# Opening of a hybrid layer: from a normed and transposed x to a transposed x whose norm factor comes later

## The chip, the cores and the metric

The kernel runs on one core of one Trainium2 chip. The metric is device time in microseconds. The kernel before takes 2043.03 us, the median of three runs (2042.36 to 2048.4).

## The reference

For x of 512 tokens by 2048 channels the layer is, with every matrix in float32:

```python
h = rmsnorm(x, norm_w)                      # x * rsqrt(mean(x*x) + eps) * norm_w, per token
z, xbc, dt_f, dt_b, q_a, kv_a, z_attn, g_ssm, g_attn = split(h @ w_in)
xbc = silu(dwconv(xbc, conv_w, conv_b))     # a centred convolution over four tokens
y = ssd_scan(...) both directions + d_skip * xs
y = group_rmsnorm(y * silu(z))
o = attention(q_a, kv_a) * silu(z_attn)
merged = sigmoid(g_ssm) * (y @ w_proj_ssm) + sigmoid(g_attn) * (o @ w_proj_attn)
out = rmsnorm(x + merged @ w_out, final_norm_w)
```

Since the norm's factor is one number per token, h @ w_in is that factor times (x * norm_w) @ w_in. The convolution mixes tokens, so there the factor must be in before it.

## The kernel before, in words

Each float32 operand is split into a high part (a cast to the matmul's format) and a low part (what the cast left over). A product is three matmuls: high by high, high by low, low by high. A matmul has a 128 x 128 stationary side and 512 columns. A weight chunk is 128 x 1024 numbers, 512 KB. SyncE's queue (SP) loads it, ScalarE (ACT) casts it to `wh`, VectorE (DVE) makes `wl`, and TensorE (PE) uses it for 24 matmuls in a plain gemm and 12 in a gate product. `wraw`, `wh` and `wl` have three buffers each.

TensorE's instructions run in the order in which the program is written. The other engines' order, and that of the DMA issues on their queues, is made by a scheduler from priorities: a gate weight's load stands up to 160 steps ahead, its split 60.

The program's stages are these.

1. Opening (L195 to L235). x is loaded in eight pieces, token by token (L208); ScalarE squares and sums each (L210); the factor is made for each group of 128 tokens (L185 to L191); x is scaled (L218, L220); 64 transposes turn it channel by channel (L225). From the turned tiles come `h_h` (L229) and `h_l` (L230), the high and low part of h with norm_w in.
2. Seven gemms on h by plain chunks (L168 to L170): `dtp`, then six for the first group of xbc. Between them `h_sums` (L723 to L743) rebuilds quarters of h from both parts and makes S1, S2, S3 and S4, the sums that the gates need, in two halves (`q`). `dt_make` (L279 to L303) makes the time steps out of `dtp`.
3. Three gates (`wz`, `wgs`, `wga`), each in two column pairs by a Strassen-Winograd scheme of seven half-size products in the order P1, P5, P6, P2, P3, P7, P4 (lines L576 to L578). A product takes four chunks and 48 matmuls. P1's chunks X are loaded by SP; when P1 has split one, POOL adds a second block of weights onto it by an accumulating DMA (L503), which makes T1, P5's operand. Y is another block; X plus Y (L670) is P6's operand, and X plus a further block (L674) is that of P4, called T4. S3 is loaded back from memory behind P5 (L445), and x21 at the end of the last pair.
4. The state scan with the other plain gemms beside it, then attention.
5. Three projections, `wps`, `wpa` and `wo`, by the same scheme; the operands S1 to S4 and x11 to x22 of the next one are loaded and split during the last products of the one before.

Row names: `xt` is x by tokens, `P` a product's bank, `wl` a low part of a weight, `T_wps` a stored sum of weights, `o_S` a stored operand of the next projection.

## Time and profile before

| | |
|---|---|
| median of three runs | 2043.03 us |
| profiled execution | 2034.87 us |
| its span | 2033.1 us |
| mean granted TensorE clock | 0.992 |
| TensorE busy | 1955.8 us, 96% |
| VectorE busy | 1465.7 us, 72% |
| ScalarE busy | 967.4 us, 48% |
| first matmul of a gemm | 32.63 us |
| first matmul of the first gate | 108.91 us |

A timeline row is start, duration, engine, line, operation, output and inputs, shapes, a count, and in brackets the idle time before it with what ended it. A row of windows is the stretch, its length, the busy time of PE, PE's weight loads, DVE, ACT and POOL, the granted clock, the share of DMA and GB/s. A group's row ends with busy time, mean ns of one, and the idle time before. A row of DMA issues ends with the KB of one and the median us from issue to landing. A matmul is issued every 0.227 us though its row says 0.39, since matmuls are pipelined.

### The profile page before, as it was taken

To read this page: it belongs to the slowest core of one execution; us is meant where nothing else is said; L and a number is where in the kernel's file an instruction comes from. 1 tells how busy PE (TensorE), PEld (TensorE's weight loads), DVE (VectorE), ACT (ScalarE), POOL (GpSimd) and SP (SyncE) were. 2 spreads that over 40 slices of the span, in tenths; PEclk is the share of its full clock that TensorE was granted. 3 is DMA by queue.
4 is the path that set the end of the run, shared out by engine and by line. 5 is a ranking of instruction groups with operands and counts; after the bars stand their busy time and mean duration, and the time that the engine had idled before them with its cause. 6 is when DMAs were issued, how large, how long until landed. Compare 5 with 4: busy or idle time off the path is not lost.

```text
span 2033.1 us, 24719 instructions
## 1 busy us (share of the span) xinstructions
PE 1955.8 (96%) x9074; PEld 1619.0 (80%) x9074; DVE 1465.7 (72%) x1946; ACT 967.4 (48%) x1352; POOL 324.7 (16%) x345
## 2 busy tenths in 40 slices
PE   6999999999999999999999989999999999999998
PEld 5878888888878778777788878888878787888886
DVE  7976676676759889799787567666677889776342
ACT  6444445444444656546546344444455345443232
POOL 0001001001032242243331101110020210100120
PEclk9999999999999999999999999999999999999999
DMA  5468658558456757687574857782387976855332
GB/s 196 161 186 207 160 130 207 161 129 207 124 182 177 229 143 203 207 243 216 167 197 148 231 157 201 207 220 87 90 220 278 315 250 242 276 210 171 114 114 83
DMA packets 166584, 378.56 MB, mean 186 GB/s; under 512 B 16000, under 2 KB 65280, under 8 KB 165888
## 3 DMA queue, kind: packets, MB, share of 16 engines
q1 hardware_dynamic: 103536, 234.13, 35.2%
q0 software_dynamic: 28096, 96.48, 21.2%
q10 hardware_dynamic: 34832, 46.38, 6.3%
q8 instruction: 71, 1.16, 0.2%
q14 instruction: 49, 0.40, 0.1%
HBM read 325.03 MB, written 98.04 MB: 208 GB/s over the span
## 4 chain that ended last, share of the span: by engine, by line
PE 72%; DVE 14%; DMA 6%; issue 4%; ACT 3%; POOL 1%; SPq 0%; ACTq 0%; DVEq 0%; POOLq 0%
PE P L577 10%; PE P L578 10%; PE P L576 10%; PE f L1539 3%; PE f L1540 3%; PE f L1538 3%; PE za L168 2%; PE za L169 2%; PE za L170 2%; PE xbc L168 2%; DVE sum L1022 2%; PE xbc L169 2%; PE xbc L170 2%; DVE wl L164 2%; DMA wraw<-wps 1%
## 5 line engine op out<-in xcount | busy, mean ns | idle before, releaser
L434 DVE TENSOR_TENSOR wl<-X,wh 128x1024 fp32r<-128x1024 f32 x152 | 185.5, 1224 | 84.8 <-ACT wh L433 84.3
L433 ACT CAST wh<-X 128x1024 fp32r<-128x1024 f32 x152 | 159.6, 1053 | 177.1 <-PE P L578 158.0
L164 DVE TENSOR_TENSOR wl<-wraw,wh 128x1024 fp32r<-128x1024 f32 (+2 forms) x148 | 173.6, 1174 | 87.4 <-ACT wh L163 84.9
L163 ACT CAST wh<-wraw 128x1024 fp32r<-128x1024 f32 (+2 forms) x150 | 144.8, 968 | 139.1 <-PE xbc L169 39.2
L434 DVE TENSOR_TENSOR wl<-wraw,wh 128x1024 fp32r<-128x1024 f32 x74 | 91.4, 1235 | 99.5 <-ACT wh L433 97.3
L168 PE MATMUL xbc<-h_h,wh 128*128 128x512 f32 x384 | 151.4, 394 | 0.0
L170 PE MATMUL xbc<-h_h,wl 128*128 128x512 f32 x384 | 149.7, 390 | 0.0
L169 PE MATMUL xbc<-h_l,wh 128*128 128x512 f32 x384 | 149.4, 389 | 0.0
L576 PE MATMUL P<-wh,h_h 128*128 128x512 f32 x384 | 149.4, 389 | 0.0
L577 PE MATMUL P<-wl,h_h 128*128 128x512 f32 x384 | 149.4, 389 | 0.0
L578 PE MATMUL P<-wh,h_l 128*128 128x512 f32 x384 | 149.4, 389 | 0.0
L434 DVE TENSOR_TENSOR wl<-Y,wh 128x1024 fp32r<-128x1024 f32 x80 | 97.9, 1224 | 69.3 <-ACT wh L433 69.1
L433 ACT CAST wh<-wraw 128x1024 fp32r<-128x1024 f32 x74 | 78.0, 1054 | 146.3 <-PE f L1540 69.5
L433 ACT CAST wh<-Y 128x1024 fp32r<-128x1024 f32 x80 | 84.2, 1053 | 114.2 <-PE P L578 88.9
L577 PE MATMUL P<-wl,S 128*128 128x512 f32 x288 | 112.4, 390 | 0.9 <-DVE wl L434 0.9
L578 PE MATMUL P<-wh,S 128*128 128x512 f32 x288 | 112.1, 389 | 0.0
L576 PE MATMUL P<-wh,S 128*128 128x512 f32 x288 | 112.0, 389 | 0.0
L168 PE MATMUL za<-h_h,wh 128*128 128x512 f32 x256 | 101.2, 395 | 0.0
L170 PE MATMUL za<-h_h,wl 128*128 128x512 f32 x256 | 99.9, 390 | 1.0 <-DVE wl L164 1.0
L169 PE MATMUL za<-h_l,wh 128*128 128x512 f32 x256 | 99.6, 389 | 0.0
L1022 DVE TENSOR_TENSOR_SCAN sum<-da,scn 128x512 f32<-128x512 f32 x64 | 87.4, 1383 | 0.0
L170 PEld LDWEIGHTS xbc<-h_h,wl 128*128 128x128 f32 x384 | 72.1, 188 | 15.3
(636 smaller groups left out, 5183.5 us busy)
## 6 DMA issues: line engine op xcount, KB each, us to landing
wraw<-wi SPq DMA_DIRECT2D x102, 512.0 KB, 4.0
T_wps<-wps POOLq DMA_DIRECT2D x32, 512.0 KB, 6.2
da<-da_d SPq DMA_DIRECT2D x64, 256.0 KB, 4.4
T_wpa<-wpa POOLq DMA_DIRECT2D x32, 512.0 KB, 8.8
wraw<-wo SPq DMA_DIRECT2D x32, 512.0 KB, 3.4
wraw<-wps SPq DMA_DIRECT2D x24, 512.0 KB, 5.4
xbc_d<-xbc ACTq DMA_DIRECT2D x24, 256.0 KB, 2.8
wraw<-wun SPq DMA_DIRECT2D x16, 384.0 KB, 3.1
```

What stands on the lines that cost most here:

```text
L163: act.copy(h, raw)
L164: (dve if ahead[0] else pool).tensor_sub(l, raw, h.bitcast(F32))
L168: pe.matmul(out, wh, xh, start=start, stop=False)
L169: pe.matmul(out, wh, xl, start=False, stop=False)
L170: pe.matmul(out, wl, xh, start=False, stop=stop)
L433: i = act.copy(hi_, raw)
L434: dve.tensor_sub(lo_, raw, hi_.bitcast(F32))
L576: pe.matmul(bs[i], xh, wh, start=(j == 0), stop=False)
L577: pe.matmul(bs[i], xh, wl, start=False, stop=False)
L578: pe.matmul(bs[i], xl, wh, start=False, stop=(j == 7))
L1022: dve.tensor_tensor_scan(sums[dd], flat(da), mask, 0.0, ALU.add, ALU.mult)
L1538: pe.matmul(acc, mh, wh, start=(start and k == 0), stop=False)
```

## The change

x now also comes as `xt`, an input laid out by channels, and is read straight into `x_t`, one tile, channel by channel; no transposes are left. `h_h` and `h_l` are made of x and norm_w, without the norm's factor. The factor (the Squares over a second load of x, then `token_factors`) is spread over a tile R by four matmuls (`factor`) in the fifth gemm; the results of the xbc gemms are multiplied by R ahead of the convolution (`xbc_done`), the time steps in `dt_make`, and the gates' results by a scale in their activation. Three gemms run interleaved while x arrives, and `dtp` is the last of the seven instead of the first. `h_sums` reads quarters of `x_t`, and `x_t` itself is stored in four parts, which the last gate pair loads back, multiplies by R and splits, so that h with its factor is there for the rest. The tiles X, Y and the others of the gates (pool `wx`) are laid out anew: X after the small ones. P1's first two weight chunks (`first_w`) are loaded into the ring `wraw` and split ahead of the second sums; those chunks of X then need no split, and their accumulation follows the load directly. `dt_make` moves behind P2 of the first pair. In `wps`, the end of `head` becomes a fill piece of its own.

```diff
+    act.dma_start(vec, a["vec"])
     act.dma_start(cst, a["cst"])
-    act.dma_start(vec, a["vec"])
...
+    so = open_pool("so", side="right", reuse_waits="tile")
+    s_op = {w: so.tile([P, 2, 8, 256], F32R, name=w) for w in ("S1", "S2", "S4")}
+    xp = open_pool("xp", side="right", reuse_waits="tile")
+    sx = open_pool("sx", reuse_waits="tile")
+
+    x_t = xp.tile([P, KT, SEQ], F32, name="x_t")
+
+    def xk(k):
+        return k % 8 // 4 * 8 + k // 8 * 4 + k % 4
...
-            nc.sync.dma_start(xt[:, cs], a["x"][t * P:(t + 1) * P, cs])
...
-            act.activation(scr, xt[:, cs], AF.Square, accum_out=ss[:, i:i + 1])
...
-    tps = [mm(), mm(), mm(), pa(), pa(), pb(), pb(), pc()]
-
-    def x_turn(k, t):
-        pe.transpose(tps[k % 8][:, t * P:(t + 1) * P], xs_t[t][:, k * P:(k + 1) * P], ident)
-
-    def x_out(k):
-        nw = vec[:, V_NORM + k:V_NORM + k + 1]
-        act.activation(h_h[:, k, :], tps[k % 8], AF.Copy, scale=nw)
-        dve.scalar_tensor_tensor(h_l[:, k, :], tps[k % 8], nw, h_h[:, k, :].bitcast(F32), ALU.mult, ALU.subtract)
-
...
+    warm_ps = pc("warm")
+    dve.memset(v_x, 1.0)
+    for _ in range(2):
+        pe.matmul(warm_ps, v_x[:, 0:P], v_x, start=True, stop=True)
+
+    ahead[0] = 1
+    firsts_i = (T_XBC + 4, T_XBC + 5, T_XBC)
+    early = [[] for _ in firsts_i]
+    for j in range(8):
+        for n, at in ((0, 0), (1, 2), (2, 4), (0, 4), (1, 6)):
+            if at == j:
+                early[n].append(wchunk(a["wi"][firsts_i[n], len(early[n])], 1024))
+        xs = x_t[:, xk(2 * j):xk(2 * j) + 2, :].rearrange("p k t -> p (k t)")
+        nc.sync.dma_start(xs, a["xt"][j])
+        for k in (2 * j, 2 * j + 1):
+            nw = vec[:, V_NORM + k:V_NORM + k + 1]
+            act.activation(h_h[:, k, :], x_t[:, xk(k), :], AF.Copy, scale=nw)
+            dve.scalar_tensor_tensor(h_l[:, k, :], x_t[:, xk(k), :], nw, h_h[:, k, :].bitcast(F32), ALU.mult, ALU.subtract)
+    early[2].append(wchunk(a["wi"][firsts_i[2], 1], 1024))
+    for k in range(KT):
+        tc.keep_in_program_order(dve.tensor_scalar_mul(x_t[:, xk(k), :], x_t[:, xk(k), :], vec[:, V_NORM + k:V_NORM + k + 1]))
+    r4, ss = few(4), few(8)
     for t in range(TT):
         for i in range(2):
+            xs = sxq("xs")
+            nc.sync.dma_start(xs, a["x"][t * P:(t + 1) * P, i * D // 2:(i + 1) * D // 2])
+            act.activation(xs, xs, AF.Square, accum_out=ss[:, 2 * t + i:2 * t + i + 1])
+        if t == 1:
+            fourth = [wchunk(a["wi"][T_XBC + 1, 0], 1024)]
...
+    def token_factors():
+        v4, rt = few(4), few(4)
+        sv = ss.rearrange("p (t i) -> p t i", i=2)
+        dve.tensor_add(v4, sv[:, :, 0], sv[:, :, 1])
+        dve.tensor_scalar(v4, v4, 1.0 / D, EPS, ALU.mult, ALU.add)
+        new = {"rt": rt, "rr": r4}
+        small_rsqrt(v4, 4, lambda n: new[n])
+        for t in range(TT):
+            dve.tensor_scalar_mul(v_x[:, t * P:(t + 1) * P], ident, r4[:, t:t + 1])
+    def factor():
+        rp = pc("rp")
+        for t in range(TT):
+            pe.matmul(rp[:, t * P:(t + 1) * P], ones, v_x[:, t * P:(t + 1) * P], start=True, stop=True)
+        act.copy(R, rp)
+        put(r_d, R)
...
+            h, l = given[m] if m < len(given) else w_split(raw)
+            if extra and m >= len(given):
...
+            w_load(t, self.w, cp, 0, 0, m)
+            if headed:
+                w_more(t, self.w, cp, 0, 1, m, LOAD_AHEAD)
...
+        s1, s3 = sxq("s1"), sxq("s3")
+        tc.keep_in_program_order(dve.tensor_sub(view4(s1), x(1, 0), x(1, 1)))
+        keep("S1", s1)
+        tc.keep_in_program_order(dve.tensor_sub(view4(s3), x(0, 0), x(1, 0)))
         put(h_d["S3"][:, cs], s3)
+        s2 = sxq("s2")
+        dve.tensor_sub(view4(s2), view4(s1), x(0, 0))
+        keep("S2", s2)
+        dve.tensor_add(view4(s1), view4(s2), x(0, 1))
+        keep("S4", s1)
+    def together(gens, order):
+        gens = {n: g_ for n, g_ in zip("ABC", gens)}
+        for i, n in enumerate(order):
+            next(gens[n])
+            yield i
+        for g_ in gens.values():
+            run(g_)
+    def xbc_done(i, p_, v=v_x):
+        dve.tensor_mul(v, p_, R)
+        o = st("xbc")
+        put(xbc_d[0][i], conv_silu(v, (0, 1, 2, 3, 16, 20)[i], o, lambda n: o))
-    for i in range(5):
-        run(xbc_gen(0, (4, 5, 0, 1, 2, 3)[i], sxt))
-        if i in (1, 3):
-            h_sums(i // 2)
-    dt_make(sxd)
...
+    firsts = [mm("xbc") for _ in range(3)]
+    order = "AAAABBBB" + "AABB" * 2 + "C" * 8 + "A" * 8 + "B" * 8 + "C" * 8
+    for i in together([gemm_steps(p_, win(t), h_h, h_l, w_) for p_, t, w_ in zip(firsts, firsts_i, early)], order):
+        pass
+    ahead[0] = AHEAD
+    h_sums(0)
+    token_factors()
+    places = [pb("xbc"), pb("xbc")]
+    run(gemm_steps(places[0], win(T_XBC + 1), h_h, h_l, fourth))
+    for i, _ in enumerate(gemm_steps(places[1], win(T_XBC + 2), h_h, h_l)):
+        if i == 2:
+            factor()
+    for i, p_ in zip((4, 5, 0, 1), firsts + places[:1]):
+        xbc_done(i, p_)
+    for q in range(2):
+        for n, (j, i) in (("x11", (0, 0)), ("x12", (1, 0)), ("x21", (0, 1)), ("x22", (1, 1))):
+            pool.dma_start(view4(h_d[n][:, q * 1024:(q + 1) * 1024]), x_t[:, 8 * q + 4 * j:8 * q + 4 * j + 4, i * 256:(i + 1) * 256])
+    v_2 = sxq("v_2")
+    xbc_done(2, places[1], v_2[:, 0:SEQ])
+    p_ = mm("xbc")
+    run(gemm_steps(p_, win(T_XBC + 3), h_h, h_l))
+    xbc_done(3, p_, v_2[:, SEQ:1024])
+    dtp = mm("dtp")
+    run(gemm_steps(dtp, win(T_DT), h_h, h_l))
+    first_w = [w_split(w_load(w_tile("w"), "wz", 0, 0, 0, m)) for m in range(2)]
+    h_sums(1)
     close_pool("sx")
+    close_pool("xp")
+    def h_part(which, i, j, q):
+        h, l = part_of(i, j, q)
+        split_into(h, l, view4(h_ops.raws[which][q]), in_order=which == "S3")
...
-    for tag, n, w in (("X", 4, 1024), ("p1", 2, SEQ), ("p5", 2, SEQ), ("u", 2, SEQ), ("pad", 2, SEQ), ("Y", 4, 1024)):
+    for tag, n, w in (("p1", 2, SEQ), ("p5", 2, SEQ), ("u", 2, SEQ), ("pad", 2, SEQ), ("X", 4, 1024), ("Y", 4, 1024)):
...
+            act.activation(o, o, f, scale=r4[:, t:t + 1])
...
+    def h_load(which, tag="w", in_order=False):
+        def f():
+            h_ops.raws[which] = []
+            for q in range(2):
+                t = w_tile(tag)
+                made = nc.sync.dma_start(t, h_d[which][:, q * 1024:(q + 1) * 1024])
+                if in_order:
+                    tc.keep_in_program_order(made)
+                h_ops.raws[which].append(t)
+        return f
+    def h_scale(which, i):
+        def f():
+            for t in h_ops.raws[which]:
+                dve.tensor_mul(view4(t), view4(t), r_back[0][:, i * 256:(i + 1) * 256].unsqueeze(1).broadcast_to([P, 4, 256]))
+        return f
+    def h_new(which, i, j):
+        return lambda: [h_part(which, i, j, q) for q in range(2)]
...
+    gates[0].hooks = {(0, "P5"): [h_load("S3", in_order=True), h_new("S3", 1, 0)], (0, "P2"): [dt_make]}
+    gates[2].hooks = {(1, "P1"): [r_load, h_load("x11"), h_scale("x11", 0), h_new("x11", 0, 0)],
+                      (1, "P2"): [h_load("x12"), h_scale("x12", 0), h_new("x12", 0, 1)],
+                      (1, "P3"): [h_load("x21"), h_scale("x21", 1)],
+                      (1, "P7"): [h_new("x21", 1, 0), h_load("x22", "X"), h_scale("x22", 1)],
+                      (1, "P4"): [h_new("x22", 1, 1)]}
+    gates[0].given[0] = first_w
     gates[0].first_columns(0)
-    run(xbc_gen(0, 3, None))
-    for p_ in gates:
+    first_pair = gates[0].pair(0)
+    for _ in range(8):
+        next(first_pair)
+    dv_ = st("dv_")
+    tc.keep_in_program_order(act.copy(dv_, dtp))
+    put(dv_d, dv_)
+    run(first_pair)
+    run(gates[0].pair(1))
...
+            fill.add("head", (lambda: (yield from wps.head_end()))())
```

On SP's queue, before, x stands first and weights follow; `wi` are the plain gemms' weights.

```order
L208 DMA xt_239<-x 128x1024 x2
L208 DMA xt_256<-x 128x1024 x2
L208 DMA xt_273<-x 128x1024 x2
L208 DMA xt_290<-x 128x1024 x2
L160 DMA wraw<-wi 128x1024 x14
L445 DMA xraw<-h_S_200 128x1024 x2
L467 DMA wraw<-wz 128x1024
L467 DMA X<-wz 128x1024 x4
L467 DMA Y<-wz 128x1024 x4
```

Now, from the queue's start to the gates:

```order
L160 DMA wraw<-wi 128x1024
L238 DMA x_t<-xt 128x1024 x2
L160 DMA wraw<-wi 128x1024
L238 DMA x_t<-xt 128x1024 x2
L160 DMA wraw<-wi 128x1024 x2
...
L160 DMA wraw<-wi 128x1024 x7
L482 DMA wraw<-wz 128x1024 x2
L482 DMA X<-wz 128x1024 x4
L482 DMA Y<-wz 128x1024 x4
L839 DMA wraw<-h_S_202 128x1024 x2
```

Weights and x alternate, two chunks of `wz` go into the ring ahead of X, and S3 (`h_S`) comes behind Y.

On VectorE at the end of the opening, now; the first row is the second low part of `first_w`, and L750 to L757 with the splits L449 between them are the second sums:

```order
L449 TENSOR_TENSOR wl<-wraw,wh 128x1024
L750 TENSOR_TENSOR s_872<-x_t 128x1024
L755 TENSOR_TENSOR s_879<-s_872,x_t 128x1024
L449 TENSOR_TENSOR S_239<-s_872,S_239 128x1024
L752 TENSOR_TENSOR s_873<-x_t 128x1024
L449 TENSOR_TENSOR S_240<-s_879,S_240 128x1024
L757 TENSOR_TENSOR s_872<-s_879,x_t 128x1024
L449 TENSOR_TENSOR S_241<-s_872,S_241 128x1024
```

Before, the second sums were begun behind the fourth gemm of xbc; now they stand behind the last weight split ahead of X's own, and L757 is the last reader of `x_t`, on whose place X now lies and for which SP's first X load waits.

On VectorE at the second column pair of `wps`, before; `wl<-X` belongs to P4, L674 is the sum for T4, L437 the split of S2, L604 P7's first sum:

```order
L674 TENSOR_TENSOR X<-X,wraw 128x1024
L434 TENSOR_TENSOR wl<-X,wh 128x1024
L437 SCALAR_TENSOR_TENSOR S__14081<-xraw,S__14081 128x1024
L434 TENSOR_TENSOR wl<-X,wh 128x1024
L674 TENSOR_TENSOR X<-X,wraw 128x1024 x2
L604 TENSOR_TENSOR p_13804<-p_13804,P_13983 128x512
```

And now, with L696 the sum for T4, L449 and L455 the splits of S1 and S2, L620 P7's first sum:

```order
L449 TENSOR_TENSOR S__13940<-xraw,S__13940 128x1024
L449 TENSOR_TENSOR wl<-Y,wh 128x1024
L449 TENSOR_TENSOR S__13940<-xraw,S__13940 128x1024
L455 SCALAR_TENSOR_TENSOR S__14047<-xraw,S__14047 128x1024 x2
L620 TENSOR_TENSOR p_13770<-p_13770,P_13949 128x512
L723 TENSOR_TENSOR kk<-kk,P_13949 128x512
L696 TENSOR_TENSOR X<-X,wraw 128x1024
L1451 TENSOR_TENSOR p_13770<-p_13770,gate 128x512
L696 TENSOR_TENSOR X<-X,wraw 128x1024 x2
L449 TENSOR_TENSOR wl<-X,wh 128x1024
L696 TENSOR_TENSOR X<-X,wraw 128x1024
```

The sums for T4, of which the first two stood ahead of S2's second split, come behind both splits of S1 and S2 and behind P7's first sum.

174 lines of the change are left out of this document (61 added, 113 removed).

## The prediction

> **What bounds the kernel now.** I read the page's busy shares first, then its chain of waits.
>
> ```profile
> PE 1955.8 (96%) x9074; PEld 1619.0 (80%) x9074; DVE 1465.7 (72%) x1946; ACT 967.4 (48%) x1352; POOL 324.7 (16%) x345
> PE 72%; DVE 14%; DMA 6%; issue 4%; ACT 3%; POOL 1%; SPq 0%; ACTq 0%; DVEq 0%; POOLq 0%
> ```
>
> TensorE is busy for 1955.8 of 2033.1 us and makes up 72% of the chain, so only the 77 us without matmuls, and matmuls that do no product of the reference, can be won. Next the timeline and the groups of the opening.
>
> ```profile
> 6.00 1.06 ACT L210 ACTIVATE scr<-xt 128x1024 f32<-128x1024 f32 x1 [2.83 <-DMA xt<-x]
> 7.60 1.06 ACT L210 ACTIVATE scr<-xt 128x1024 f32<-128x1024 f32 x1 [0.45 <-DMA xt<-x]
> 7.85 0.17 DVE L837 TENSOR_SCALAR small<-vec 128x8 f32<-128x8 f32 x1 [7.85 <-DMA vec<-vec]
> 12.00:16.00 4.00, 3.06 (x14) 2.31 (x12) 3.12 (x14) 3.40 (x7) 0.00 (x0) 1.00 1.02 419
> L225 PE MATMUL mm<-cst,xt 128*128 128x128 f32 x24 | 6.4, 432 | 19.4 <-DVE xt L220 19.4
> 32.63 0.48 PE L168 MATMUL dtp<-h_h,wh 128*128 128x512 f32 x1
> 108.91 0.39 PE L576 MATMUL P<-wh,h_h 128*128 128x512 f32 x1
> ```
>
> The first two halves of x land at 6.0 and 7.6 us and the queue then moves 419 GB/s (last column), that is 512 KB each 1.25 us. The transposes wait 19.4 us for normed tiles, and the first matmul of a gemm is at 32.63. From there to the first gate product P1 at 108.91 lie seven gemms of 48 matmuls, 336 in 76.28 us: 0.227 us each with no gap. Thus the whole opening can be shortened by at most some 24 us.
>
> **The opening.** Removed: 64 transposes and the wait for the norm. The seven gemms stay, in another order; matmuls are as many. What must now precede the first matmul is a weight load (6.0), the first piece of x (7.6) and its cast; these rows price cast, low part and weight split:
>
> ```profile
> 25.79 1.84 ACT L229 ACTIVATE h_h<-mm,vec 128x512 fp32r<-128x512 f32 x3
> 26.51 2.07 DVE L230 SCALAR_TENSOR_TENSOR h_l<-mm,vec,h_h 128x512 fp32r<-128x512 f32 x3 [1.29 <-ACT h_h L229]
> 36.40 1.22 DVE L164 TENSOR_TENSOR wl<-wraw,wh 128x1024 fp32r<-128x1024 f32 x1
> ```
>
> h_h costs 0.61 us, so the first matmul is at about 8.3. The norm's weights, which arrive at 7.85 behind another constant, now go first on their queue. The order takes four steps (12 matmuls, 2.7 us) of gemm A, then gemm B, whose weights are fourth in the queue, behind x0 and x1: landed at 7.6 + 2 x 1.25 = 10.1, cast (1.05, a row below) by 11.2, low part by 12.4. B's third matmul waits for that, as if all had run without a gap from 12.4 - 14 x 0.227 = 9.2. After that x pieces land each 1.25 to 2.5 us against 2.7 us for four steps, and DVE's 16 low parts of 0.70 and six splits of 1.22 (18.5 us) fit into the 32.7 us of the three gemms. So 9.2 us, if the clock is full.
>
> ```profile
> 27.32 2.82 PE L225 MATMUL mm<-cst,xt 128*128 128x128 f32 x12
> 31.40 1.04 PE L225 MATMUL pb<-cst,xt 128*128 128x128 f32 x8
> ```
>
> The granted clock (third column from the end of the window row above) reads 1.00 from the start, yet the same transposes took 0.235 us after the wait and 0.13 at the end. By the column the start is 9.2; by the transposes the first 12 to 24 matmuls could take twice as long (2.7 us more for 12), a part of it inside the wait for B, which makes 11.0. I take 10.1, the middle. The Trainium skill, "TensorE: Matmul & The Clock Gate" (Part 1: The HAM clock gate), says that half rate is the default and some 3.4 us of sustained work lifts it, and would have the start at 11.0; the transposes agree with it, the column doesn't. New matmuls are two warming ones, before any data, and four that spread the token factors late in the fifth gemm, 0.7 us with a change of banks. P1 starts at s = 10.1 + 76.3 + 0.7 = 87.1 (86.2 to 88.0): **21.8 us gained there** (20.9 to 22.7). The Squares (eight at 1.06 us, ACT, after x) and the factors' small operations lie beside matmuls and are done by about 51 us; the four matmuls that use them come at 10.1 + 4.1 x 10.9 = 55. If that margin of 4 us were gone, PE would wait for as long as they are late, some 2 us by two weight casts that can stand ahead of them on ACT; I take 0.
>
> **The start of the gates.** Before, it looks like this:
>
> ```profile
> 95.47 3.35 SPq L467 DMA_DIRECT2D X<-wz  x4
> 107.44 2.01 POOL L503 DMA_DIRECT2D X<-wz  x2 [83.40 <-DVE wl L434]
> 120.47 1.05 ACT L433 CAST wh<-X 128x1024 fp32r<-128x1024 f32 x1 [1.64 <-DMA X<-wz]
> 123.94 1.05 ACT L433 CAST wh<-X 128x1024 fp32r<-128x1024 f32 x1 [1.45 <-DMA X<-wz]
> 127.48 2.94 ACT L433 CAST wh<-X 128x1024 fp32r<-128x1024 f32 x3 [2.48 <-DMA X<-wz]
> 126.31 0.50 PE L577 MATMUL P<-wl,S 128*128 128x512 f32 x1 [0.45 <-DVE wl L434]
> 132.51 0.39 PE L576 MATMUL P<-wh,S 128*128 128x512 f32 x1
> X<-wz SPq DMA_DIRECT2D x4, 512.0 KB, 6.6
> X<-wz POOLq DMA_DIRECT2D x4, 512.0 KB, 11.7
> 105.90 2.35 DVE L434 TENSOR_TENSOR wl<-X,wh 128x1024 fp32r<-128x1024 f32 x2
> wraw<-wi SPq DMA_DIRECT2D x102, 512.0 KB, 4.0
> wraw<-wo SPq DMA_DIRECT2D x32, 512.0 KB, 3.4
> 100.00:120.00 20.00, 20.00 (x90) 16.56 (x89) 12.23 (x13) 8.88 (x10) 3.63 (x4) 1.00 1.03 311
> ```
>
> The four X loads are issued 13.4 us ahead of P1, and the accumulating DMAs that make T1 out of them decide P5: its chunks come 3.5 us apart instead of 2.7, and PE loses 1.8 us by P6, whose first matmul is at 132.5 where two products of 48 matmuls from 108.9 would end at 130.7.
>
> In the change X lies where x_t was. The first X load waits for the last reader of x_t, the fourth of the second sums (with two low parts of S1 and S2 between them, six DVE operations), and these stand in DVE's order behind the low parts of the two first weights. The second of these needs the buffer that the first chunk of the last opening gemm frees, at s - 5.4. From there: cast 1.05 and low part 1.22, then the six at 1.13 from start to start (two took 2.35 in the row above), and 0.2 to issue: s - 5.4 + 9.3 = s + 3.9. P1's first two chunks have their weights and run until s + 5.4. The third needs X2, the third load: 4.0 us for the first as weights take in a row above and 2.5 for two more, then cast and low part: s + 3.9 + 6.5 + 2.3 = s + 12.7. **PE waits 7.3 us** (5.5 if loads land in 3.4 us as the quickest kind does on the page and DVE's six run closer, 8.5 if they take the 6.6 of X's own row). Behind X on SP's queue stand the Y loads, S3 and further weights, all as late.
>
> What such a wait costs beyond itself the trace shows late in the kernel:
>
> ```profile
> 1602.00:1606.00 4.00, 0.34 (x2) 0.00 (x0) 1.98 (x2) 1.04 (x1) 0.00 (x0) 0.84 1.03 420
> 1606.00:1608.00 2.00, 1.57 (x4) 1.28 (x5) 2.00 (x3) 1.05 (x1) 0.00 (x0) 0.50 0.91 303
> 1608.00:1610.00 2.00, 2.00 (x6) 1.53 (x5) 1.97 (x5) 0.00 (x0) 0.98 (x2) 0.50 0.89 277
> 1606.43 0.79 PE L577 MATMUL P<-wl,S__13444 128*128 128x512 f32 x1 [4.09 <-DVE wl L434]
> ```
>
> After 4.09 us of idling the clock is 0.50 for about 5 us: 11 or 12 matmuls at 0.43 us, **2.3 us more** (1.5 to 2.5). P1 ends at about s + 20.5 instead of s + 10.9.
>
> T1's first accumulation can go as soon as X0 has landed (s + 8), but it shares the DMA engines with X2, X3, Y and S3. It landed 11.7 us after issue in the median before, so it is there at s + 20; the chunks then come 3.5 us apart against 2.72: 2.9 us lost at P5 (0 if all have landed, 4.5 if they queue up), where 1.8 stood. Together the gates' start gives back 7.3 + 2.3 + 2.9 - 1.8 = **10.7 us** (5.2 to 13.7).
>
> **Moved work without a price.** dt's chain goes from the opening to P3 and P7 of the first pair; its four reciprocals and table load end about when P7's first weights are split, so 0, or 1.5 if that margin is gone. The last gate pair restores four parts of h instead of one, 14 DVE operations more:
>
> ```profile
> 480.00:520.00 40.00, 40.00 (x178) 33.15 (x177) 29.51 (x28) 20.06 (x23) 3.45 (x4) 1.00 0.53 128
> 520.00:560.00 40.00, 40.00 (x178) 33.12 (x177) 27.43 (x29) 19.95 (x24) 3.46 (x4) 1.00 0.59 159
> ```
>
> 14 x 1.2 = 17 us go into DVE's 80 - 56.9 = 23 us of idle time: 0.
>
> **Late, at P4 of wps's second column pair,** the order changes too: all four additions for T4 now stand behind the splits of S1 and S2 and behind the first sum of P7, and their loads behind those splits.
>
> ```profile
> wraw<-wps SPq DMA_DIRECT2D x24, 512.0 KB, 5.4
> 1657.06 0.33 SPq L467 DMA_DIRECT2D wraw<-wps  x1
> 1663.90 0.33 SPq L467 DMA_DIRECT2D wraw<-wps  x1
> 1668.52 1.46 SPq L467 DMA_DIRECT2D wraw<-wps  x2
> 1675.82 1.23 DVE L674 TENSOR_TENSOR X<-X,wraw 128x1024 f32<-128x1024 f32 x1 [2.79 <-DMA wraw<-wps]
> 1678.26 0.49 PE L576 MATMUL P<-wh,x__13532 128*128 128x512 f32 x1 [1.37 <-ACT wh L433]
> 1681.23 0.80 PE L577 MATMUL P<-wl,x__13532 128*128 128x512 f32 x1 [2.48 <-DVE wl L434]
> ```
>
> Before, the loads go out at 1657.1, 1663.9 and 1668.5; P4's third chunk waits 1.37 + 2.48 us and the clock falls after it, 6.2 us in all. P7 began at 1678.3 - 1.4 - 72 x 0.227 = 1660.5. Now, counted from there: DVE has P3's sums and gates, the low parts of P7's weights and the four splits of S1 and S2 in a row, the last of which needs a load that the first split frees (issued at 4.5, landed and cast at 9.5). The three loads leave behind the last three splits at 6.8, 7.9 and 10.6 us; the third lands 3.4 to 5.4 later, and its addition (1.2) and the low part behind it (1.2) end at 16.4 to 18.4, though P4's first chunk wants that low part at 10.9: a wait of 5.5 to 7.5, plus 2.3. That is 8.7 in place of 6.2: **2.5 us lost** (2 gained if the last split isn't late, so that the third load leaves with the second; 4 lost if loads take 7 us).
>
> **Sum.** 21.8 - 10.7 - 2.5 = 8.6 us. On the profiled execution's 2034.87 us this gives 2026.3; that execution lies 8.2 us below the median of the runs, 2043.0, and the forecast is set against the median: **2034.4 us**. Its own bounds: at best 22.7 - 5.2 + 2 = 19.5 gained, at worst 20.9 - 13.7 - 4 - 1.5 = 1.7.
>
> **Rivals.** (a) X lies only under the half of x that is read first, as the change's name says, and its loads don't wait for the second sums: P1 has no wait, 21.8 - 2.5 = 19.3 gained, 2024 us. For it: the first half's sums stand four gemms (44 us) earlier. Against it: the order puts X behind those sums, which read the second half of x_t. (b) P1's delay gives the accumulations time, so that P5 waits for nothing, and the late loads of wps come quickly: 21.8 - 7.3 - 2.3 + 1.8 + 2 = 16.0, 2027 us. For it: from X0's landing to P5 there are 12.5 us, and 11.7 was the median; against it, Y and S3 now come in the same 12.5 us. (c) The gates' start is bound by DMA: Y, S3, P2's first weights and the accumulations, counted twice as they read and write, are some 9 MB, which at the 311 GB/s of the stretch before takes 29 us from s + 9, so that the last accumulation lands at s + 38 instead of s + 30: P5 loses 8 us more, and late loads cost 4 instead of 2.5: 8.6 - 8 - 1.5 = -0.9, 2044 us, no change. For it: 1.03 of DMA share in that stretch; against: it held writes that are gone. (d) Slower: DVE becomes the bound of the last gate pair. A multiplication by a broadcast factor has no row before; from 23 us of added work on PE waits. At twice the 1.22 us of a plain one, the eight make the 14 operations 8 x 2.4 + 6 x 1.2 = 27 us: 4 us over, and as the restores come in bunches behind P1, P2, P3 and P7, up to four waits of some 2 us more with a cold restart of 2.3 after each long one, 16 in all. Then 8.6 - 16 = -7.4, 2050 us. Against: every plain operation of that size takes 1.22 in this trace, whatever its inputs.
>
> **Chances.** Forecast 0.50, (a) 0.07, (b) 0.14, (c) 0.20, (d) 0.09. About 0.3%, 6.1 us, is what a measurement of this kernel can tell from no change; the forecast lies 2.5 us beyond that, so a fifth of its chance is "same". Faster: 0.40 + 0.07 + 0.14 = 0.61; same: 0.10 + 0.19 + 0.03 = 0.32; slower, most of (d) and the end of (c): 0.07. The range leaves out about a fifth, (d), half of (a) and the end of (c): 2025 to 2044.
>
> **What would show it.** First gemm matmul at 8 to 9 us, P1 at 86 to 88; X loads issued about 4 us after P1's start and a wait of 7 us at its third chunk with clock 0.50 behind it; P5's chunks 3.5 us apart; P4 of wps's second pair waiting at its first chunk. It is wrong if P1's third chunk hardly waits (a), if P5 waits for nothing (b) or over 8 us (c), or if PE waits for DVE in the last gate pair (d).

## The result, and the profile after

The changed kernel takes 2055.49 us, the median of seven runs (2050.82 to 2056.66). The kernel before, run beside it, takes 2042.51 us (seven runs, 2041.42 to 2048.4). The ratio is 1.0061, with a 95% interval of 1.0046 to 1.0075: slower by about 12.5 us, where 8.6 us less was forecast.

The profiled execution of the change took 2050.82 us (span 2048.4, mean granted clock 0.984). The busy shares and the chain of waits on its page read almost as before; DMA has risen from 6% to 9% of the chain and PE has fallen from 72% to 70%.

```profile
PE 1960.4 (96%) x9022; PEld 1616.8 (79%) x9022; DVE 1469.7 (72%) x1958; ACT 977.1 (48%) x1354; POOL 328.6 (16%) x351
PE 70%; DVE 13%; DMA 9%; ACT 4%; issue 3%; POOL 1%; ACTq 0%; SPq 0%; DVEq 0%; POOLq 0%
```

To find the place, each matmul from P1 on was set beside its twin in the profile of before, and the difference of their starts read as a lag (negative: the change is ahead). The second column takes another profile of the unchanged kernel (e7 below), whose span is 2043.4 instead of 2033.1 us.

| place in the program | start in the change, us | lag to the first profile of before | to the second |
|---|---|---|---|
| first matmul of P1 | 90.83 | -18.1 | -18.1 |
| late in P1 | 108.99 | -7.6 | -7.6 |
| P2 | 159.69 | -5.7 | -5.7 |
| scan's first sums | 575.49 | -3.4 | -3.5 |
| late in attention | 1500.39 | +1.2 | -8.4 |
| P7 of wps's second pair | 1667.82 | +4.5 | -5.8 |
| P4 there, after its first chunk | 1693 | +19.6 | +9.4 |
| end of P4 | 1699 | +13.1 | +3.6 |

Three places can be read in both columns: the opening gained 18.1, the gates' start gave back 12.4, and P4 of wps cost 9 us net (4.5 to 13.1, -5.8 to 3.6; before itself loses 6 us there, by which the lag falls again). Between 575 and 1667 the two columns disagree by 10 us although both are the same kernel before; that part is taken up in e7.

The timeline of the opening of the change, on PE:

```profile
1.46 3.78 PE L228 MATMUL warm<-v_x 128*128 128x512 f32 x4 [1.46 <-DVE v_x L226]
7.63 0.79 PE L168 MATMUL xbc<-h_h,wh 128*128 128x512 f32 x1 [2.39 <-ACT h_h L241]
9.44 0.63 PE L168 MATMUL xbc<-h_h,wh 128*128 128x512 f32 x1
9.86 0.63 PE L169 MATMUL xbc<-h_l,wh 128*128 128x512 f32 x1
13.28 0.63 PE L168 MATMUL xbc<-h_h,wh 128*128 128x512 f32 x1
14.02 0.39 PE L170 MATMUL xbc<-h_h,wl 128*128 128x512 f32 x1
14.25 0.40 PE L168 MATMUL xbc<-h_h,wh 128*128 128x512 f32 x1
49.87 0.50 PE L168 MATMUL xbc<-h_h,wh 128*128 128x512 f32 x1 [0.74 <-ACT wh L163]
90.83 0.39 PE L591 MATMUL P<-wh,h_h 128*128 128x512 f32 x1
```

The first matmul of a gemm is at 7.63. Matmuls start 0.43 us apart up to 13.7 and 0.23 apart from there. At 49.87 PE waits for the fourth gemm's weight. P1 starts at 90.83.

The start of the gates, from the timelines of SP and PE:

```profile
94.64 1.75 SPq L482 DMA_DIRECT2D X<-wz  x4
103.72 0.80 PE L591 MATMUL P<-wh,h_h 128*128 128x512 f32 x1 [7.29 <-ACT wh L449]
106.00 0.63 PE L591 MATMUL P<-wh,h_h 128*128 128x512 f32 x1
109.90 0.40 PE L592 MATMUL P<-wl,h_h 128*128 128x512 f32 x1
159.69 0.50 PE L592 MATMUL P<-wl,h_h 128*128 128x512 f32 x1 [1.63 <-DVE wl L449]
547.29 0.50 PE L592 MATMUL P<-wl,h_h 128*128 128x512 f32 x1 [1.07 <-DVE wl L449]
```

X's loads go out at 94.64, and P1's third chunk waits 7.29 us for its weight; matmuls run at half rate until about 109.4. The last two rows are a weight of P2 and one of the last gate pair, each a little late.

The late place, from PE's, SP's, ACT's and DVE's timelines (L462 loads the operands of the next projection, L449 and L454/L455 split them, L696 is the sum for T4), with a row of windows and, last, the DMA issue at 1674.14:

```profile
1686.44 0.80 PE L591 MATMUL P<-wh,x__13498 128*128 128x512 f32 x1 [10.34 <-ACT wh L449]
1689.29 0.80 PE L592 MATMUL P<-wl,x__13498 128*128 128x512 f32 x1 [2.06 <-DVE wl L449]
1660.78 9.69 SPq L482 DMA_DIRECT2D Y<-wpa  x3
1671.87 0.33 SPq L462 DMA_DIRECT2D xraw<-o_S  x1
1674.14 11.45 SPq L482 DMA_DIRECT2D wraw<-wps  x4
1656.46 1.04 ACT L449 CAST S__13940<-xraw 128x1024 fp32r<-128x1024 f32 x1
1680.59 1.06 ACT L454 ACTIVATE S__14047<-xraw 128x1024 fp32r<-128x1024 f32 x1 [11.23 <-DMA xraw<-o_S]
1670.62 1.22 DVE L449 TENSOR_TENSOR S__13940<-xraw,S__13940 128x1024 fp32r<-128x1024 f32 x1
1681.67 1.23 DVE L455 SCALAR_TENSOR_TENSOR S__14047<-xraw,S__14047 128x1024 fp32r<-128x1024 f32 x1 [6.42 <-ACT S__14047 L454]
1684.01 1.22 DVE L696 TENSOR_TENSOR X<-X,wraw 128x1024 f32<-128x1024 f32 x1
1672.00:1680.00 8.00, 4.09 (x19) 3.05 (x17) 3.25 (x3) 0.00 (x0) 1.19 (x3) 0.97 0.99 343
wraw<-wps SPq DMA_DIRECT2D x1, 512.0 KB, 9.6
```

Read from the end: P4's first chunk waits 10.34 us for a cast, and the cast for the sum L696 at 1684.01. Two chains end just ahead of this sum, and either alone would have held it about as long. On DVE it stands behind the second split of S2 (L455), which can't begin before 1681.65; DVE idles 6.42 us ahead of that split. And its own operand, the first load of `wps`, left at 1674.14 and took 9.6 us, so that it landed at 1683.8.

Both chains lead back to the low parts of S1 on DVE, since the raw operands and these weights share one ring of three buffers. S2's second load left at 1671.87, when the low part of S1's first half ended (1670.62 + 1.22 = 1671.84), and landed at 1680.6, 8.7 us later, in a stretch in which DMA is busy 0.99 of the time (the row of windows). The load of `wps` left at 1674.14, when the low part of S1's second half ended (1674.11). The cast of the first half was done by 1657.5; its low part could have run from then on, but was kept in order behind other splits and sums, and DVE idled 1.56 and 3.55 us in the meantime.

### The profile page after: what moved, and what is told of

The parts are those of the page before. It is cut to its first block, busy times and chain, and to the rows that moved or that the text cites. A ratio compares the mean times of both kernels' runs of the same rounds, so it can differ in the third digit from the quotient of the medians.

```text
span 2048.4 us, 24682 instructions
## 1 busy us (share of the span) xinstructions
PE 1960.4 (96%) x9022; PEld 1616.8 (79%) x9022; DVE 1469.7 (72%) x1958; ACT 977.1 (48%) x1354; POOL 328.6 (16%) x351
## 4 chain that ended last, share of the span: by engine, by line
PE 70%; DVE 13%; DMA 9%; ACT 4%; issue 3%; POOL 1%; ACTq 0%; SPq 0%; DVEq 0%; POOLq 0%
PE P L592 9%; PE P L593 9%; PE P L591 9%; PE f L1616 3%; PE f L1617 3%; PE f L1615 3%; PE xbc L168 2%; PE xbc L169 2%; PE za L168 2%; PE za L169 2%; PE xbc L170 2%; PE za L170 2%; DVE sum L1098 2%; DVE wl L449 2%; DVE wl L164 1%
## 5 line engine op out<-in xcount | busy, mean ns | idle before, releaser
L449 DVE TENSOR_TENSOR wl<-X,wh 128x1024 fp32r<-128x1024 f32 x150 | 182.6, 1222 | 83.1 <-ACT wh L449 82.6
L449 ACT CAST wh<-X 128x1024 fp32r<-128x1024 f32 x150 | 157.7, 1054 | 169.6 <-PE P L593 134.0
L449 DVE TENSOR_TENSOR wl<-wraw,wh 128x1024 fp32r<-128x1024 f32 x76 | 93.7, 1233 | 102.3 <-ACT wh L449 102.2
L449 ACT CAST wh<-wraw 128x1024 fp32r<-128x1024 f32 x76 | 80.1, 1054 | 151.8 <-PE f L1617 72.2
L449 DVE TENSOR_TENSOR wl<-Y,wh 128x1024 fp32r<-128x1024 f32 x80 | 97.8, 1222 | 59.6 <-ACT wh L449 59.6
L449 ACT CAST wh<-Y 128x1024 fp32r<-128x1024 f32 x80 | 83.9, 1052 | 108.5 <-PE P L593 80.9
L591 PEld LDWEIGHTS P<-wh,h_h 128*128 128x128 f32 x384 | 72.6, 189 | 22.9 <-ACT wh L449 7.7
L168 PEld LDWEIGHTS xbc<-h_h,wh 128*128 128x128 f32 x384 | 73.5, 191 | 20.2 <-ACT h_h L241 4.0
```

The lines of the kernel that those rows point to most:

```text
L168: pe.matmul(out, wh, xh, start=start, stop=False)
L449: made = act.copy(hi_, raw), dve.tensor_sub(lo_, raw, hi_.bitcast(F32))
L591: pe.matmul(bs[i], xh, wh, start=(j == 0), stop=False)
```

## The experiments

The three suspects are the pin that puts the low parts of splits in program order (e1, e5), the second sums ahead of X's loads (e2), and the slow first matmuls (e3); e4 takes all three. The theory formed from the traces was that the late order comes from the pin; the rival, for the time as a whole, that the opening's gain is simply lost again somewhere behind the gates.

### e1: the low part of a split isn't pinned

In the change `split_into` keeps both halves of a split, ACT's cast and DVE's low part, in program order where it is asked to; before, only the cast was kept. Here the cast alone is kept, as before, but for S2, whose cast stays free as in the change; the new splits of S3 behind P5 of the first gate keep both.

```diff
-                for m in made:
+                for m in made[:in_order]:
                     tc.keep_in_program_order(m)
```

> The changed kernel, but of a projection's operand splits only the cast is pinned to the program's order, as before, and not the low part on VectorE too. Theory (the pinning put the sums for T4 behind both splits of S1 and S2): P4 of wps's second column pair no longer waits 10.3 us at its first chunk but as in the kernel before (some 4 us at its third), with one cold restart in either; lag added there 11 us falls to 0 to 2, so 9 to 11 us less than the changed kernel, about 2045 us. Rival (the wait is S2's slow load, 8.7 us, or the traffic around it, and not the order): 5 us or more of it stays, 2050 us.

Measured: 2043.86 us (12 runs), before beside it 2040.02 (28 runs); ratio 1.0016, 0.9999 to 1.0033. Against the change's 1.0061 that is 0.0045, some 9 us less. Its two longer waits at and behind P4, DVE's splits of S1 and first sum, and SP's loads of `wps`:

```profile
1681.69 0.50 PE L592 MATMUL P<-wl,x__13498 128*128 128x512 f32 x1 [0.60 <-DVE wl L449]
1694.96 0.50 PE L591 MATMUL P<-wh,x__13774 128*128 128x512 f32 x1 [2.29 <-ACT wh L449]
1661.37 2.35 DVE L449 TENSOR_TENSOR S__13940<-xraw,S__13940 128x1024 fp32r<-128x1024 f32 x2
1669.56 1.23 DVE L696 TENSOR_TENSOR X<-X,wraw 128x1024 f32<-128x1024 f32 x1 [1.23 <-DMA wraw<-wps]
1663.75 2.60 SPq L482 DMA_DIRECT2D wraw<-wps  x2
```

The wait of 10.34 us is gone, and not only down to the some 4 us of before: P4 waits 0.60 us. The low parts of S1 run 9 us earlier, the loads of `wps` leave 10 us earlier, and the first sum for T4 stands 14 us earlier. What is late next is the operand of the product behind P4, the first of wpa, whose first chunk now waits 2.3 us (the second row); before, and in the change, there is no such wait, since P4's own comes first.

### e2: the second sums ahead of the last gemms

```diff
+    h_sums(1)
     v_2 = sxq("v_2")
...
     first_w = [w_split(w_load(w_tile("w"), "wz", 0, 0, 0, m)) for m in range(2)]
-    h_sums(1)
...
-        nc.sync.dma_start(v, dv_d)
+        tc.keep_in_program_order(nc.sync.dma_start(v, dv_d))
```

The second sums come two gemms earlier. The load in the last lines, dt's, is kept in program order, so that it stays behind its own store.

> The changed kernel with the second sums written ahead of the sixth gemm, so that x_t's last reader stands ahead of the low parts of the first gate weights (and the load of the time steps pinned where it was). Theory (X's loads wait for that reader): X is issued 5 to 10 us ahead of P1, P1 has no wait of 7.3 us and no half clock after it; P5 may wait for its accumulations some 2 to 3 us more than now: 7 to 10 us less than the changed kernel, about 2047 us. Rival (the gates' start is bound by DMA): the wait only moves to P5, 0 to 3 us less, 2053 us.

Measured: 2043.62 us (12 runs), ratio 1.0018, 1.0004 to 1.0033, some 9 us less than the change. SP's queue and PE in this kernel:

```profile
87.43 2.50 SPq L482 DMA_DIRECT2D X<-wz  x4
92.17 0.39 PE L591 MATMUL P<-wh,h_h 128*128 128x512 f32 x1
99.06 0.50 PE L591 MATMUL P<-wh,h_h 128*128 128x512 f32 x1 [1.30 <-ACT wh L449]
```

X's loads now leave 4.7 us ahead of P1 instead of 3.8 us behind its start, and the wait falls from 7.29 to 1.30 us. The time is as expected; the loads were expected 5 to 10 us ahead, with no wait left.

### e3: a third warming matmul

```diff
-    for _ in range(2):
+    for _ in range(3):
         pe.matmul(warm_ps, v_x[:, 0:P], v_x, start=True, stop=True)
```

> The changed kernel with three warming matmuls instead of two, so that TensorE is busy until about 7.1 us and idle for 0.5 instead of 2.4 us before the first gemm. Theory (the first 13 matmuls run at half rate because the two warming ones end too early): they run at 0.227 us each, P1 comes 2.5 us earlier, 2 to 3 us less in all. Rival (what runs first is at half rate whatever ran before, or the clock needs data-like work): 0.

Measured: 2050.71 us (six runs), ratio 1.0054, 1.0034 to 1.0074. The intervals of this and of the change overlap almost wholly, so the times don't resolve a difference. The trace does show one: with six passes of warming instead of four, PE idles 0.89 us instead of 2.39 before the first gemm, the first matmuls start 0.23 us apart, and from the fifteenth matmul to P1's start the kernel is 2.1 to 2.5 us ahead of the change.

```profile
1.46 5.13 PE L228 MATMUL warm<-v_x 128*128 128x512 f32 x6 [1.46 <-DVE v_x L226]
7.47 0.50 PE L168 MATMUL xbc<-h_h,wh 128*128 128x512 f32 x1 [0.89 <-ACT h_h L241]
8.84 0.40 PE L168 MATMUL xbc<-h_h,wh 128*128 128x512 f32 x1
9.08 0.40 PE L169 MATMUL xbc<-h_l,wh 128*128 128x512 f32 x1
```

### e4: all three

The edits of e1, e2 and e3 together.

> All three edits together. Theory (three separate losses): they add up, 19 to 23 us less than the changed kernel, about 2034 us, some 8 us less than the kernel before. Rival (a time won at the gates' start is given back by later waits, since the projections' order hangs on the same queues): 10 to 14 us less, 2043 us, as the kernel before.

Measured: 2033.69 us (11 runs), ratio 0.997, 0.9955 to 0.9985. Beside e9, against other runs of before, the same kernel took 2036.73 us (12 runs), ratio 0.9976, 0.996 to 0.9992. Both times it is faster than before. From 1.0061 to 0.997 are 18.6 us; the three alone gave 9, 9 and 1.4, so within the 4 us or so that each of these differences is uncertain by they add up: the two large losses are at two places that don't touch. P1 starts at 90.34, 18.6 us ahead of before, and yet only 5 to 6 us arrive at the end.

### e5: the pin alone, in the kernel before

The kernel before, with nothing changed but that the low part is kept in program order with the cast (and nothing is kept for S2, as in the change; e1 leaves that so too, so it isn't what e1 recovers).

```diff
-            i = act.copy(hi_, raw)
-            dve.tensor_sub(lo_, raw, hi_.bitcast(F32))
+            i = act.copy(hi_, raw), dve.tensor_sub(lo_, raw, hi_.bitcast(F32))
...
-                    tc.keep_in_program_order(i)
+                    for m in i if which != "S2" else ():
+                        tc.keep_in_program_order(m)
```

> The kernel before with nothing of the change but its way of pinning the operands' splits: the low part on VectorE is pinned as well as the cast (S2's cast not at all, as in the change). Its order at P4 of wps's second pair is then that of the change. Theory (the pinning alone makes the late wait): a wait of some 10 us at P4's first chunk, 7 to 11 us slower than before, about 2050 us. Rival (the wait needs the shifted start of the change, by which loads meet in the queues): 0 to 4 us slower.

Measured: 2051.29 us (12 runs), before beside it 2040.51 (23 runs), ratio 1.0044, 1.0027 to 1.006: the pin costs 9 us (5.5 to 12) without any of the rest. The rows of PE, SP and ACT are those of the change in other numbers:

```profile
1687.77 0.79 PE L576 MATMUL P<-wh,x__13532 128*128 128x512 f32 x1 [9.27 <-ACT wh L433]
1674.32 0.33 SPq L444 DMA_DIRECT2D xraw<-o_S  x1
1681.92 1.06 ACT L435 ACTIVATE S__14081<-xraw 128x1024 fp32r<-128x1024 f32 x1 [10.11 <-DMA xraw<-o_S]
1673.07 1.22 DVE L433 TENSOR_TENSOR S__13974<-xraw,S__13974 128x1024 fp32r<-128x1024 f32 x1
```

The low part of S1 ends at 1674.29, S2's second load leaves at 1674.32 and lands 7.6 us later, and P4 waits 9.27 us. Taken away from the change (e1) and added to the kernel before (e5), the pin is worth the same 9 us; that it makes the late loss is shown.

### e6 and e8: a later opening

e4 with 12 and with 28 warming matmuls in place of 3, which hold up the first gemm.

```diff
-    for _ in range(3):
+    for _ in range(12):
         pe.matmul(warm_ps, v_x[:, 0:P], v_x, start=True, stop=True)
```

> The kernel with all three edits (0.997 of before), started late: twelve warming matmuls instead of three, so that the first gemm begins some 15 to 16 us later and everything behind it is as it was. This measures what a us at P1 is worth at the end. Theory (TensorE is the bound from there on, and what the opening wins is kept): 15 to 16 us slower than that kernel, about 2049 us. Rival (later stages wait for queues that don't start earlier, and a good part of the opening's gain is lost there): 5 to 10 us slower, about 2041 us.

Measured: 2034.0 us, ratio 0.9976, 0.9963 to 0.999: no different from e4. But the edit did not do what it was for. The first gemm matmul came at 13.01 instead of 7.74, and P1 at 90.49 instead of 90.34: the lag of 5.3 us was 2.15 at 49.4 and 0.25 at the factor's matmuls (58.7). So this run says nothing of what a us at P1 is worth. It says that the opening of e4 has 5 us of slack: 1.9 us lay in matmuls at half rate (the lag is 3.4 once e4 has left it), and 3.2 in the waits at 49 us (1.08 and 0.53) and at the factor (0.79) with the wider spacing behind them, which are not there when the first gemm starts later.

```profile
13.01 0.79 PE L168 MATMUL xbc<-h_h,wh 128*128 128x512 f32 x1
```

> As e4_all_three, with 28 warming matmuls in place of 3; the whole result is computed. In the run with 12 of them the first gemm matmul came 5.3 us later (13.0 for 7.7), and by the factor's matmuls at 58.7 this had shrunk to 0.25 us: the opening had that much slack, and P1 was not moved. Each warming matmul takes 0.96 us there, so 16 more put the first gemm matmul at about 28.4, 20.7 us behind that of e4. Theory (TensorE sets the time from P1 on, so a us at P1 is a us at the end): of the 20.7 us some 3 to 6 fall into the waits of the opening (slow first matmuls, 49 us, the factor at 59), P1 comes at 105 to 107, 15 to 17 us later than in e4, but the second sums and the X loads are no later than before against P1, so the P1 wait of 1.3 us goes; time 2048 to 2050. Rival (the gates' start is paced by loads and sums that don't depend on the first matmul, so a later P1 finds them done and loses less): P1's and P5's waits shrink and the time rises by 5 to 10 us only, 2039 to 2044.

Measured: 2048.06 us (12 runs), before beside it 2039.73 (17 runs), ratio 1.0037, 1.0023 to 1.005. Against e4's 0.997 that is 0.0067, 13.7 us, with about 4 us of uncertainty.

```profile
105.06 0.39 PE L591 MATMUL P<-wh,h_h 128*128 128x512 f32 x1
100.32 1.75 SPq L482 DMA_DIRECT2D X<-wz  x4
111.95 0.49 PE L591 MATMUL P<-wh,h_h 128*128 128x512 f32 x1 [1.29 <-ACT wh L449]
```

P1 comes 14.7 us later than in e4 and the end 13.7 us later, as the theory had it: in this kernel a us at P1 is about a us at the end. The other part of the expectation fell. The P1 wait did not go, it is 1.29 us as in e4, and X's loads leave 4.74 us ahead of P1 in both. They follow P1 about, whatever the second sums do. On SP's queue they stand behind the second load of `first_w`, which waits for the buffer that the last opening gemm's first chunk frees; that this is what holds them fits the 4.7 us but wasn't tried.

### e7: the kernel before, once more

> The kernel before once more, for a second profile of it. Theory (its first profiled execution, 8 us below the median, had fewer of the stretches at half rate than most): more stretches at a clock of 0.50 between 560 and 1600 us, span 2036 to 2045 us. Rival (the two traces are alike and the change itself adds such stretches): the same stretches, span 2033 us.

Measured: 2045.18 us, span 2043.4, clock 0.987, against 2034.87, 2033.1 and 0.992 in the first profile. A window of the first profile of before, and then of the second, at about the same place of the program (the second is 6 to 8 us behind there):

```profile
996.00:1000.00 4.00, 4.00 (x19) 3.30 (x18) 3.91 (x5) 2.01 (x3) 4.00 (x4) 1.00 0.37 114
```

```profile
996.00:1000.00 4.00, 4.00 (x12) 3.12 (x11) 2.41 (x6) 1.97 (x4) 2.97 (x3) 0.50 0.16 57
```

The same program runs at clock 0.50 in one execution where the other has 1.00. Between 20 and 2020 us the clock records hold 27 us at half rate in the first profile and 48 in the second, in stretches of 3.4 or 6.8 us. The lag between the two grows by 0.5 to 2.2 us at about eight such places (596, 660, 826, 880, 960, 995, 1380 and 1615 us) and reaches 10.8 us. Lags between two single profiles behind the scan's start therefore say nothing about the change within some 10 us; the places with a wait of their own do.

### e9 and e10: the head of wps in one piece, and e4 again

The change makes the end of wps's head a filler piece of its own, which lays out the filler work beside scan and attention anew; the prediction gave it no price. e9 is e4 with that undone, e10 is e4 itself.

```diff
-        def head_end(self):
-            return self.second(1, self.p1[1], lambda i: sum_tile("p5"), None, "P2b")
+            yield from self.second(1, b, lambda i: sum_tile("p5"), None, "P2b")
...
-            fill.add("head", (lambda: (yield from wps.head_end()))())
```

> As e4_all_three, with the end of wps's head back inside the head, as before the change, so that the filler work beside the scan and attention is laid out as before. The whole result is computed. From P1 on e4 is 18.6 us ahead of before in the traces but only 6.3 us in the medians; 6 us go at the gates' waits. In attention the wait for the scaled row of probabilities takes 6.0 us in e4, 3.6 and 5.2 in the two kernels derived from it, and 1.8 and 1.4 in two profiles of before. Theory (the new layout of the filler work makes the attention waits): those waits return to about 1.5 to 2 us, and the time falls by 2 to 4 us against e4, 2030 to 2032. Rival (the waits come from weights that land late by chance, whatever the layout): waits of 3 to 6 us, time within 2 us of e4, 2032 to 2036.

> The kernel of e4_all_three once more, beside e9_head_in_one, for its second profile and for more runs. Both theories: 2032 to 2036, ratio 0.996 to 0.998. If the attention wait depends on chance it differs from the 6.0 us of the first profile by a microsecond or more.

Measured: e9 2033.46 us, ratio 0.9966 (0.9951 to 0.9981); e10 2036.73 us, ratio 0.9976 (0.996 to 0.9992); before beside both 2040.32 (23 runs). The intervals overlap: a gain of 1 to 3 us by e9 is neither shown nor excluded. The wait for the scaled row of probabilities in attention (600 to 1600 us), of before's first profile, and then of e9:

```profile
PE pb L1298 <- DVE pr L1287: 1.8, 3, 0.8
```

```profile
PE pb L1372 <- DVE pr L1361: 3.5, 3, 2.2
```

The wait for `pr` (us in total, times, longest) stays at 3.5 us; in e10 it is 3.2, where the same kernel had 6.0 in its first profile. So most of its spread is chance, and the layout of the filler work doesn't make it. That it is above before's 1.4 and 1.8 in every profile of the changed kernels stays unexplained.

## Why the prediction was wrong

**The opening: right in its mechanism, 3.7 us too large.** Predicted were a first matmul at about 8.3, P1 at 87.1 and 21.8 us gained. Measured were 7.63, 90.83 and 18.1. The difference lies at three places. The term "equivalent gap-free start 10.1" was 0.7 too low: counted back from the first matmul at full rate, the sixteenth (14.25 less 15 x 0.227), it is 10.8. Twelve matmuls took 7.63 to 13.28, 5.65 us instead of 2.7, which is 2.9 more, and the wait for gemm B that was part of the 10.1 hardly came. The Trainium skill, "TensorE: Matmul & The Clock Gate" (Part 1: The HAM clock gate), was weighed in the prediction for its 11.0, and these rows agree with its rule that half rate is the default until sustained work lifts it, here 6.3 us after the first matmul of a gemm. The clock column's 1.00, which spoke for 9.2, stands on no record there (see the last section). Not in the sum were the two short waits at 50 us (0.74 and 0.53), 1.8 us with the wider spacing behind them. And the factor's matmuls cost 1.9 us with their wait of 0.76, where 0.7 was put. e3, with full rate from the start, has P1 2.4 us earlier; in e6 and e8, with a later start, the waits at 50 and 59 us of e4 are gone, 3.2 us.

**The gates' start: right.** The X loads were put at 3.9 us behind P1's start and left 3.81 behind; the wait at the third chunk was put at 7.3 and took 7.29, with a half-rate stretch behind it. With the restart P1 gave back 10.5 us (predicted 9.6), the products behind it 1.9 (1.1): 12.4 instead of 10.7. P5's share was not where it was put: its chunks waited 0.30 and 0.76 us, and P2's weight 1.63. e2 removed most of it, so its cause, the second sums ahead of X's loads, is shown; what holds X's loads after that was not tried.

**Moved work without a price: 2.3 us instead of 0.** In the last gate pair one weight's low part was late by 1.07 us, and the first sums of the scan by 1.52 instead of 0.74. Rival (d) had 16 us of waits in that pair; it lost 1.4.

The wait of the scan's first sums isn't stable. In the nine profiles of kernels with the change it took 1.3 to 5.2 us, 2.9 in the mean; in the three with the opening of before it is 0.74 each time. Rows of ACT in before, and then of ACT and PE in e1:

```profile
576.08 0.62 ACT L922 CAST c_h<-CT 128x512 fp32r<-128x512 f32 x1 [1.90 <-DMA CT<-xbc_d]
577.46 0.38 ACT L312 COPY daT<-pb 128x256 f32<-128x256 f32 x1
```

```profile
575.71 0.62 ACT L998 CAST c_h<-CT 128x512 fp32r<-128x512 f32 x1 [3.70 <-DMA CT<-xbc_d]
576.24 0.37 ACT L328 COPY daT<-pb 128x256 f32<-128x256 f32 x1
576.66 2.08 PE L334 MATMUL pa<-daT,cst 128*128 128x128 f32 x8 [5.05 <-ACT daT L328]
```

`daT` is what PE waits for, and ahead of it on ACT stands a cast that waits for a load, `CT`. Before, this cast began 1.9 us after ACT's last work and ahead of the matmuls whose result `daT` copies; in e1 the result was there at 571.6 and the cast held the copy until 576.24. That is read from the traces; no run moved the cast.

**The late P4 of wps is the step that failed most.** The prediction saw the new order and put the wait at 5.5 to 7.5 us with a loss of 2.5 net, at worst 4. Measured were 10.34 + 2.06 us of waiting and 9 net (e1 and e5, by medians; 8.6 to 9.4 in the table). The mechanism was the one described: the last split of S2 needs a load that a split of S1 frees, the sums stand behind it, and their loads behind the splits. The sizes in it were off. Counted from 1665.2 (where P4's wait begins, 1676.1, less P7's 48 matmuls, 10.9) S2's load was put at 4.5 us and landed and cast at 9.5. It left at 6.7, since the low part of S1 is itself held in order behind other splits and sums, and was cast at 16.5, since it took 8.7 us to land instead of about 4. The loads for the sums were put at 6.8, 7.9 and 10.6 and at 3.4 to 5.4 us of landing; the first of them left at 8.9 and took 9.6. The prices are those of the quickest weight loads and of a median over the whole program; here four loads for wpa and four for wps went out within 25 us, with DMA at 0.99. The bound "4 lost if loads take 7 us" was too tight because the loads' lateness was not carried into everything behind them.

Of the 21 us between the forecast and the result, 6.5 lie in this step, 3.7 in the opening, 1.7 at the gates' start and 2.3 in the moved work; some 7 are left.

Of the reason for that order the prediction had nothing: it took the order as it was and did not find that one line of the change, the loop that pins both halves of a split, makes it. That line costs all of what e1 recovers.

**The rest, some 7 us, is only partly named.** With the measured terms, 18.1 - 12.4 - 2.3 - 9 = -5.6, while the medians say -12.5. The waits ahead of the value products (`vp`) and for the probabilities (`pr`) took 8.0 us in the change (4.5 and 3.5) against 5.0 and 4.2 in the two profiles of before, which is 3 to 4 of it. The scan's first sums waited 1.52 us in the change's profile, and 2.9 in the mean of all nine, so the medians probably hold more of that than the 2.3 above. In the change's profile two low parts come 1.09 us late at 1850.5 and 0.74 at 1863.3, and both columns lose 1.3 to 1.8 us between 1705 and 1870. The mean granted clock was 0.981 to 0.984 in the change's seven runs, and 0.990 in the median of before's; the two long waits explain a part, and why the rest of the kernel also has more half-rate stretches than before is open. e4, without the long waits, still has 0.987, and arrives only 5 to 6 us ahead though P1 is 18.6 ahead: some 6 us go in the gates' smaller waits; the 6 us that before loses at P4 of wps are gained, but 5 to 8 are lost again at wpa's first product (2.3 to 3.2 us of waiting and a half-rate stretch; e4, e9 and e10); 2 to 6 go in the waits of `vp` and `pr`. What is left was not traced to a place.

**The cases.** None of the rivals on record gives 2055: (d), the only one on the slower side, stood at another place and at 2050. The chance of slower, 0.07, came mostly from that one mechanism; the late term, whose low end went by rows of another stretch, should have had the wider range.

## What to carry to other kernels

A helper that pins an instruction in program order pins all it returns: when such a helper grows from one instruction to two, look at every place that calls it, as far as the other end of the kernel. The price of a load that a chain of work waits for is read from loads in the same stretch under the same traffic, not from the median of its kind, and its lateness is carried through everything that stands behind its consumer. Gains made at the start of a kernel are easily lost behind it: even with both large losses mended, 18.6 us at P1 became 5 to 6 at the end, in good part by waits of 1 to 3 us, some with a stretch at half rate behind them.

## What was not expected of the hardware

The column of granted clock reads 1.00 in the opening, while matmuls start 0.43 us apart. The same window of the change, and then of e4:

```profile
8.00:12.00 4.00, 4.00 (x10) 2.81 (x10) 3.87 (x6) 3.74 (x6) 0.00 (x0) 1.00 1.03 423
```

```profile
8.00:12.00 4.00, 3.72 (x10) 2.78 (x10) 3.87 (x6) 3.74 (x6) 0.00 (x0) 0.64 1.03 423
```

Ten matmuls in 4 us, where 17 fit at 0.23: from their spacing the clock is half in both. The column is a mean over the trace's clock records, and time without a record counts as 1.00. In the change the first record begins at 13.9 us, where the spacing changes; in e4 at 5.7, and there the column falls to 0.64. In the kernel before the first record begins at 31.1 us, so the prediction's 1.00 "from the start" was an empty stretch, and the slow transposes beside it were the evidence. Ahead of the first record, only the spacing tells the rate.

A short warm-up doesn't fix the rate of what follows: four passes and 2.39 us of idling left the first 13 matmuls at half rate (7.63 to 13.7). Of the profiles with six passes, those of e3, e9 and e10 had none at half rate, with 0.89, 1.76 and 0.93 us of idling, and that of e4 eight, with 1.34: the idle time alone doesn't decide it.

Half-rate stretches of 3.4 or 6.8 us come and go between executions of one program at fixed places of it, and move the time of the same kernel by 10 us (2033.1 and 2043.4 us of span). The Trainium skill, "TensorE: Matmul & The Clock Gate" (Part 1: The HAM clock gate), says that the window in which activity is counted runs freely and that the number of slow matmuls varies from run to run; the two profiles of before, with 27 and 48 us at half rate, agree with the second. A term under 10 us that has no wait of its own in a trace can therefore be judged by medians of a dozen runs alone, and these are uncertain by some 3 us here.
